# SBUF buffers placed on 128-byte lines, and the convolution layers' weight splits and lateness constants set anew, in a six-layer f32 network on one core

## The chip, the cores and the metric

One core of a Trainium2 chip runs the whole program in one launch. The metric is device time in microseconds (us) of one execution, as the median of several runs.

## The reference

The reference takes 256 tokens of width 1024 in float32 through two blocks. The first has four mixers, in the order convolution (A0), attention (B), short convolution (C), convolution (A1), each around a residual. The second has two layers of a token mixer (M0, M1) and a feed-forward part (F0, F1). The change bears mostly on the convolution mixer:

```python
def conformer_conv_mixer(h, w_in, conv_w, conv_b, ln_g, ln_b, w_out):
    proj = h @ w_in
    val, glu_gate, z = jnp.split(proj, 3, axis=-1)
    u = val * jax.nn.sigmoid(glu_gate)
    u = causal_depthwise_conv(u, conv_w) + conv_b      # 31 taps, 2048 channels
    u = jax.nn.silu(layer_norm(u, ln_g, ln_b))
    return (u * jax.nn.silu(z)) @ w_out
```

## The kernel before

Activations lie with the features on the partitions: a tensor of width 1024 is 8 chunks of 128 partitions by 256 tokens. Every weight matrix is cut into tiles of 128 x 1024, which SP loads into `wr`.

A float32 product is made in one of two ways (`need` and `dense`). **Split**: ACT rounds the tile to `wh` (type fp32r), VectorE or GpSimd subtracts to get the rest `wl`, and TensorE does three fp32r matmuls for each 128 x 256 chunk, `wh` with `hh`, `wh` with `hl` and `wl` with `hh`, where `hh` and `hl` are the same split of the activations. **Native**: the tile is used as loaded, with one float32 matmul for each chunk, which the trace records as two matmul rows (`hn,wr`). A native tile gives ACT, VectorE and GpSimd nothing to do. `NATIVE_A` names the pairs of tiles in a convolution layer that are native: numbers 0 to 15 are the 16 pairs for value and gate, 16 to 23 the 8 pairs for z. Pair 0 is native whatever the table says.

The outputs of a layer come from `Out`: the same three matmuls, with `ph` and `pl` (the split of a layer's inner activations, 8 buffers of 128 x 256) as moving operand, into the PSUM tiles `po`.

In a convolution layer each of the 16 chunks of 128 channels has 31 taps. `POOL_TAPS` says how many of them ACT and GpSimd do: ACT scales a shifted copy into `tap`, GpSimd adds it to `C`. VectorE does the others in PSUM (`po<-U,vec,po`). Then `sums` has TensorE add up `C` and `sq` over the channels, for the layer norm, and only after all 16 chunks can `mean_rstd` (a power on GpSimd, `q`) and with it the layer's output matmuls begin.

The order on each engine isn't written by hand. `program` records operations with a due time (`G.late`, `G.rush`); `Graph.schedule` plays them through a table of estimated durations and takes, for each engine that is free, the ready operation with the earliest due time. Constants such as `CONV`, `SPLIT_LATE`, `LEAD`, `URGENT`, `MOD_LATE` shift due times. Where an operation has two engines to choose from (`FLEX`, for `wl` in the layers named), the planner picks. Where TensorE has nothing ready and too little work in its current stretch, the planner puts in a matmul of zeros, `idle<-idle`, to keep the engine's clock up; `WARM` is a margin of that rule. `Graph.issue` makes the tiles in pools and issues the instructions in the planned order.

```python
        with G.late(-LEAD):
            a.activation(h, w, AF.Copy)
            (dp if flex[0] else v).tensor_tensor(l, w, h.bitcast(F32), op=OP.subtract)
```

`issue` is the helper line of all operations, so every row of the profile has line 494. Here is what the change touches.

Of the kernel before, what the change touches and what calls it, by code (L numbers as in the profile page):

```python
# [8 lines left out]
F32 = mybir.dt.float32  # L9
F32R = mybir.dt.float32r  # L10
BF = mybir.dt.bfloat16
I32 = mybir.dt.int32
# [3 lines left out]

TABLE = {AF.Exp: "exp", AF.Sigmoid: "sigmoid", AF.Silu: "silu", AF.Sin: "sin", AF.Ln: "ln"}
FIFO = 99
DEBUG = []


# [99 lines left out]
class Graph:  # L121
# [87 lines left out]
    def schedule(self):  # L209
# [68 lines left out]
        def blocked(o, e, t):  # L278

            end = t + dict(o.choices)[e]  # L280
            for w, k, i in soon[e]:
                if t < w < end - self.HOLD[1] and w < t + self.HOLD[0] and not ops[i].done and k < o.key[0] - self.HOLD[2] and room(ops[i]) is None:
                    return True
            return False

        def pick(e, t):
# [8 lines left out]
            if e == "ACT":  # L295
                best = None
                for k, i in h:
                    o = ops[i]
                    if o.done:
                        continue  # L300
                    kk = k[0] + (self.TABLE_COST if o.table and o.table != table else 0.0)
                    if best is None or (kk, i) < best[0]:
# [45 lines left out]
        while left or events:  # L348
            for e in ENG:
# [3 lines left out]
                if o is None and e == "PE" and left and self.warm is not None and self.ops[self.warm[1]].done:  # L353
                    if t > latest + 50.0:
                        self.stuck()
                    turn(t)
                    if load >= (self.DOWN if warm else self.UP) + self.WARM:
                        push((tick + 1) * self.TICK + 0.01, "engine", "PE")
# [43 lines left out]
                for j in users[o.i]:  # L402
# [5 lines left out]
                    if waits[j] == 0:  # L408
                        push(max(at[j], t), "ready", w)
                        if w.hurry and e2 in self.HOLDS:  # L410
                            soon[e2].append((max(at[j], t), w.key[0], j))
            if DEBUG and t >= DEBUG[0]:
                DEBUG.pop(0)
                for e in ENG:
# [16 lines left out]
                    break  # L431
        self.time = t

    TABLE_COST = 6.0
    WARM = 0.2
    HOLD = 0.6, 0.1, 5.0
    HOLDS = ("DVE",)

    def idle_op(self, tag):
# [14 lines left out]
    def stuck(self):  # L454
# [5 lines left out]
            lines.append(f"{tag}: {own}")  # L460
        raise RuntimeError("\n".join(lines))


    def issue(self, tc, ctx, pools):
        nc = tc.nc
        ctx.enter_context(tc.manual_schedule())
        made = {n: ctx.enter_context(tc.tile_pool(name=n, bufs=1, **kw)) for n, kw in pools.items()}
        eng = {"PE": nc.tensor, "DVE": nc.vector, "ACT": nc.scalar, "Pool": nc.gpsimd, "DMA": nc.sync}
        count = {}
        for o in self.order:  # L470
            if o.group is not None:
                count[id(o.group)] = count.get(id(o.group), 0) + 1

        def real(a):
            return a.real() if isinstance(a, View) else a
        for o in sorted(self.order, key=lambda o: o.start):
            for b in o.bufs:
                if b.real is None:
                    tag = b.tag if b.slot is None else f"{b.tag}{b.slot}"
                    b.real = made[b.pool].tile(b.shape, b.dtype, name=b.name, tag=tag, bufs=1)  # L480
            if o.fn == "transfer":
                continue
            args = [real(a) for a in o.args]
            kw = {k: real(x) for k, x in o.kw.items()}
            if o.fn == "matmul":
                b = o.outs[0].buf
                kw["start"] = not b.started
                kw["stop"] = True
                b.started = True
                if o.group is not None:  # L490
                    count[id(o.group)] -= 1
                    kw["stop"] = count[id(o.group)] == 0
                kw["skip_group_check"] = True
            getattr(eng[o.eng], o.fn)(*args, **kw)  # L494
# [34 lines left out]
def cost(eng, fn, out, ins, args, kw):  # L529
# [21 lines left out]
    if fn in ("max", "match_replace"):  # L551
# [7 lines left out]
PICKED = -3.0e38  # L559
THRESHOLDS = list(range(1, 17)) + [int(np.ceil(16.0 * 2.0 ** (3.0 * j / 16.0) - 1e-9)) for j in range(1, 16)]  # L560
ALPHA = 4.0 ** 0.25
SLOTS = {"wr": 5, "wh": 6, "wl": 6, "wa": 2, "big": 5, "t1": 8, "t2": 4, "few": 12, "ph": 4, "pl": 4, "pT": 2, "msk": 3,
         "row": 1, "pd": 2, "po": 4, "pa": 2}
RESERVE = {"wr": FIFO, "wh": FIFO, "wl": FIFO, "wa": FIFO, "pd": FIFO}
NATIVE_A = {0, 1, 3, 6, 7, 8, 10, 12, 14, 16, 18, 20, 21}
POOL_TAPS = [2, 13, 9, 11, 14, 12, 8, 17, 19, 9, 9, 12, 9, 10, 17, 27]
LEAD = 4.45
CONV = 33.45
SPLIT_LATE = 37.42
TAIL = 4  # L570
HEADS = 0.0
KA_FIRST = True
URGENT = 7.99
APPLY = 0.0
RAW_C = 1
X_FIRST = 1
X_LATE = 988
WARM = True
SWAP = True
PRELOAD = True  # L580
MOD1 = 'm'
MOD_STEP, MOD_LATE = 4.0, 5
MOD0_STEP, MOD0_LATE = 5.0, 30
ACC_A = set()
ACC_OUT = set()
ACC_LEAD = 3.37
RUSH_TAIL = 0.0
SUMS_LATE = 1.5
LAST_APART = True
FLEX_SUM = True  # L590
FLEX_HL = False
FLEX = "aoc"


def program(G, A, V):
# [68 lines left out]
    def need(src, kind="split"):  # L664
        with G.late(-3 * LEAD):
            w = G.tile("weights", [128, 1024], F32, "wr", "wr")
# [5 lines left out]
        if kind == "acc":  # L672
            with G.late(-LEAD - ACC_LEAD):
                a.activation(h, w, AF.Copy)
# [4 lines left out]
            return [h, l]  # L679
        with G.late(-LEAD):  # L680
            a.activation(h, w, AF.Copy)
# [130 lines left out]
    idle = const([128, 128], "idle", BF)  # L812
    if WARM:
        G.warm = idle, len(G.ops)
# [101 lines left out]
    def residual(out, gain=None, i0=0, late=0.0, raw="split"):  # L916
# [4 lines left out]
        def on_chunk(c, ps, done):  # L921
            with G.rush(URGENT):
                v.tensor_tensor(x[:, c], x[:, c], ps, op=OP.add)
# [8 lines left out]
        if gain:  # L932
            with G.rush(URGENT):
                rr, rs = rms_root(ss)
# [92 lines left out]
    def layer_a(j, raw):  # L1027
# [12 lines left out]
        def conv(c):  # L1040

            u, o = U[:, c % 8], at(C, c)
            b = vc("a_conv_b", j * 16 + c)
            d0 = 31 - POOL_TAPS[c]
            with G.late(CONV):
                if d0 < 31:
# [23 lines left out]
                a.activation(sq, o, AF.Square)  # L1070
                with G.late(-CONV, (), 2.0 if c < 15 else 0.5):
                    sums(st, 0, o, grp, 2048)
# [15 lines left out]
        def kind_of(p):  # L1088
            return "native" if p in NATIVE_A else "acc" if p in ACC_A else "split"

# [11 lines left out]
        G.marks.append(G.last_pe)  # L1102
        with G.rush(URGENT):
            m = mean_rstd(st, 1e-6)
        flex[0] = "o" in FLEX
        out = Out(16)
        for c in range(16):
            n1, n2 = t1("n1"), t1("n2")
            with G.rush(URGENT if c < 2 else 0):
                v.tensor_tensor(n1, at(C, c), m[0], op=OP.subtract)  # L1110
# [55 lines left out]
    def layer_b(raw):  # L1166
# [94 lines left out]
        for gi in range(4):  # L1261
# [15 lines left out]
            for i in range(4):  # L1277
                h = 4 * gi + i
                ps = pair(A["b_in"][h], A["b_in"][16 + h])
                with G.rush(HEADS):  # L1280
                    qk_head(h, ps, (vt, zs))
                    if h < 14:
                        gated(h)
                if h == 15:
                    zgate(2)
                    with G.rush(HEADS):
                        gated(14)
# [56 lines left out]
    def residual_norm(out, l, gi, gain, shift, nxt):  # L1344
# [13 lines left out]
        def on_chunk(c, ps, done):  # L1358
            with G.rush(URGENT):
                v.scalar_tensor_tensor(x[:, c], ps, mod(l, gi, c), x[:, c], op0=OP.mult, op1=OP.add)  # L1360
# [24 lines left out]
    def mixer(l):  # L1385
# [184 lines left out]
        for h in range(4):  # L1570
            with G.rush(HEADS):
                head_b(h)
# [3 lines left out]
        for h in range(4, 8):  # L1576
            with G.rush(HEADS):
                head_b(h)
# [5 lines left out]
        for i in range(8):  # L1584
            gate(i)
            with G.rush(HEADS):
                head_a(i)
# [76 lines left out]
    with G.rush(URGENT):  # L1664
        rr, rs = rms_root(ss)
    with G.late(APPLY):
        rms_apply(rs, "a_norm", 0, SPLIT_LATE)
    raw = m, rr, rs
# [4 lines left out]
    mark()  # L1673
    raw = residual(layer_c(raw), "a_norm", 8, SPLIT_LATE, "native")
    mark()
# [9 lines left out]
def emit(tc, A, V):  # L1685
    G = Graph(SLOTS, RESERVE)
    program(G, A, V)
# [141 lines left out]
```

## Time and profile before

| what | value |
|---|---|
| median of 3 runs | 1830.97 us (1830.06 to 1831.11) |
| the profiled execution, its own time | 1831.1 us |
| its span, first to last instruction | 1829.3 us |
| TensorE matmul busy in the span | 1799.9 us, 98% |
| VectorE, ScalarE, GpSimd busy | 1487.1, 1117.5, 417.6 us |
| mean granted clock of TensorE | 0.991 |

The profiled execution's time is 1.8 us above its span. A matmul's duration in the rows runs from its start to the modelled end of its pipeline, so back-to-back matmuls overlap; what one costs is the distance from its start to the next one's start. The stages by time are: head to 14.7 us, A0 to 249.9, B to 549.9, C to 789.2, A1 to 1013.5, M0 to 1225.1, F0 to 1418.1, M1 to 1628.7, F1 to the end.

### The profile page before, as it was taken

Reading aid. Unit: us, or ns where it says so; the run is one execution under the profiler, and the core shown is the slowest. Engines: PE = TensorE matmul, PEld = TensorE weight load, DVE = VectorE, ACT = ScalarE, POOL = GpSimd, SP = SyncE. Lnnn points to the kernel's source line nnn. Section 1 sums busy time; section 2 is a strip of 40 time slices with the busy share of each in tenths; the row PEclk is TensorE's granted clock in tenths of the full one; section 3 lists DMA queues with packets and bytes.
Section 4 is the critical chain, followed back from the end, with each engine's and each line's share of the span. In section 5 each row is a group of like instructions: output and inputs, shape, how many; then the busy total and the mean of one; then the engine's idle time right before and its main releaser. Section 6 shows DMA issues by size and latency. Waiting matters only on the chain.

```text
span 1829.3 us, 38072 instructions
## 1 busy us (share of the span) xinstructions
PE 1799.9 (98%) x14515; PEld 1725.9 (94%) x14515; DVE 1487.1 (81%) x3260; ACT 1117.5 (61%) x1986; POOL 417.6 (23%) x478
## 2 busy tenths in 40 slices
PE   9999999999999999999999999999999999999999
PEld 8889999999989999999989989999999989999998
DVE  7998988877778676679998798799987685687776
ACT  6777665655544444477775658856555568766554
POOL 4899511001010011049983000010001000000000
PEclk9999999999999999999999999999999999999999
DMA  7344556887754655544445656657885433446661
GB/s 251 116 152 133 184 195 209 263 254 247 246 163 150 185 173 173 174 139 139 139 168 168 214 185 200 223 182 257 289 268 160 151 122 118 137 150 210 194 189 55
DMA packets 107176, 334.95 MB, mean 183 GB/s; under 512 B 12785, under 2 KB 13169, under 8 KB 106993
## 3 DMA queue, kind: packets, MB, share of 16 engines
q1 hardware_dynamic: 106992, 332.52, 56.7%
q8 instruction: 114, 1.87, 0.4%
q14 instruction: 70, 0.57, 0.1%
HBM read 331.43 MB, written 1.05 MB: 182 GB/s over the span
## 4 chain that ended last, share of the span: by engine, by line
PE 79%; DVE 10%; ACT 4%; DMA 2%; POOL 2%; issue 2%; SPq 0%; POOLq 0%; DVEq 0%; ACTq 0%
PE pd L494 49%; PE po L494 22%; PE pa L494 7%; DVE po L494 4%; DVE wl L494 2%; PE idle L494 1%; POOL C L494 1%; ACT wh L494 1%; ACT L494 1%; DMA wa<-in_w_ada 1%; DVE IQ L494 1%; DMA wr<-in_a_in 1%; ACT tap L494 1%; DVE m L494 0%; DMA pi<-in_pos 0%
## 5 line engine op out<-in xcount | busy, mean ns | idle before, releaser
L494 ACT ACTIVATE wh<-wr 128x1024 fp32r<-128x1024 f32 x478 | 502.8, 1058 | 387.0 <-PE pd L494 239.0
L494 PE MATMUL pd<-hh,wh 128*128 128x256 f32 x2456 | 689.7, 283 | 3.6 <-DVE hh L494 1.1
L494 DVE TENSOR_TENSOR wl<-wr,wh 128x1024 fp32r<-128x1024 f32 x458 | 565.4, 1241 | 148.5 <-ACT wh L494 146.3
L494 PE MATMUL pd<-hh,wl 128*128 128x256 f32 x2456 | 678.2, 281 | 1.4 <-POOL wl L494 1.4
L494 PE MATMUL pd<-hl,wh 128*128 128x256 f32 x2456 | 677.9, 280 | 0.3 <-DVE hl L494 0.3
L494 PEld LDWEIGHTS pd<-hh,wh 128*128 128x128 f32 x2456 | 463.8, 189 | 9.3 <-issue 1.7
L494 PEld LDWEIGHTS pd<-hl,wh 128*128 128x128 f32 x2456 | 461.4, 189 | 2.0 <-issue 0.7
L494 PEld LDWEIGHTS pd<-hh,wl 128*128 128x128 f32 x2456 | 459.5, 189 | 3.0 <-POOL wl L494 1.8
L494 POOL TENSOR_TENSOR C<-C,tap 128x233 f32<-128x233 f32 (+15 forms) x364 | 276.0, 784 | 42.2 <-ACT tap L494 32.3
L494 PE MATMUL po<-ph,wh 128*128 128x256 f32 x904 | 254.6, 283 | 0.3 <-DVE ph L494 0.2
L494 PE MATMUL po<-ph,wl 128*128 128x256 f32 x904 | 253.8, 282 | 0.0
L494 PE MATMUL po<-pl,wh 128*128 128x256 f32 x904 | 251.6, 283 | 0.1
L494 DVE SCALAR_TENSOR_TENSOR po<-U,vec,po 128x251 f32<-128x251 f32 (+19 forms) x532 | 217.6, 472 | 2.2
L494 PE MATMUL pd<-hn,wr 128*128 128x256 f32 x768 | 175.2, 382 | 1.3 <-DVE U L494 1.3
L494 PEld LDWEIGHTS po<-ph,wh 128*128 128x128 f32 x904 | 170.2, 188 | 1.2 <-DVE ph L494 0.3
L494 ACT ACTIVATE tap<-U,vec 128x227 f32<-128x227 f32 (+17 forms) x364 | 156.2, 482 | 24.2 <-POOL C L494 16.6
L494 PEld LDWEIGHTS po<-ph,wl 128*128 128x128 f32 x904 | 170.4, 188 | 0.0
L494 PEld LDWEIGHTS po<-pl,wh 128*128 128x128 f32 x904 | 168.9, 189 | 0.4 <-DVE pl L494 0.3
L494 PEld LDWEIGHTS pd<-hn,wr 128*128 128x128 f32 x768 | 142.6, 190 | 19.3 <-DVE U L494 1.6
L494 POOL TENSOR_TENSOR r<-r,neghalf 128x4 f32<-128x4 f32 (+1 forms) x22 | 27.8, 1262 | 302.3 <-DVE r L494 244.9
L494 POOL TENSOR_TENSOR acc<-acc,x 128x256 f32<-128x256 f32 x12 | 9.3, 777 | 336.6 <-DVE x L494 336.0
L494 POOL TENSOR_TENSOR wl<-wr,wh 128x1024 fp32r<-128x1024 f32 x20 | 50.3, 2513 | 154.4 <-ACT wh L494 154.3
(273 smaller groups left out, 2649.7 us busy)
## 6 DMA issues: line engine op xcount, KB each, us to landing
wr<-in_a_in SPq DMA_DIRECT2D x96, 512.0 KB, 3.6
wa<-in_w_ada SPq DMA_DIRECT2D x192, 256.0 KB, 4.0
wr<-in_w_up SPq DMA_DIRECT2D x88, 512.0 KB, 4.4
wr<-in_c_in SPq DMA_DIRECT2D x64, 512.0 KB, 3.6
wr<-in_m_in SPq DMA_DIRECT2D x64, 512.0 KB, 4.1
wr<-in_b_in SPq DMA_DIRECT2D x48, 512.0 KB, 4.5
wr<-in_w_dn SPq DMA_DIRECT2D x44, 512.0 KB, 4.4
wr<-in_a_out SPq DMA_DIRECT2D x32, 512.0 KB, 4.4
```

What stands on the lines that cost most here:

```text
L494: getattr(eng[o.eng], o.fn)(*args, **kw)
```

## The change

`place` makes every tile's row a whole number of 128-byte lines, and a tile of a few words at the head of three pools shifts what follows: the pool of constants by 32 bytes, the weights and the pools behind them by 64 bytes each. The constants, `hh` and `hl` among them, begin 32 bytes behind a line in both programs, and `wr`, `wh`, `wl` 96 bytes behind one in both. `ph` and `pl` begin on a line before (offset 0) and 32 bytes behind one after; the big activation buffers, the `t1` buffers and others move from offset 96 to 32. The reserve `dynamic_dma_scratch_size` falls from 16,384 to 1,024 bytes per partition, which pays for one more `wl` (7) and one more `t2` (5).

`NATIVE_A` has 15 numbers where it had 13; as pair 0 is native anyway, 12 pairs that counted become 15, so in each of the two convolution layers three more pairs (six tiles) are native. `FLEX` is empty: every `wl` is now VectorE's. One more tap of chunk 14 goes to ACT and GpSimd. The rest are due-time constants and margins.

```diff
+LINE = 128
+PHASES = {"const": 8, "weights": 16, "big": 16}
...
-    TABLE_COST = 6.0
-    WARM = 0.2
-    HOLD = 0.6, 0.1, 5.0
+    TABLE_COST = 0
+    WARM = 0.51
+    HOLD = 0.71, 0.14, 5.08
...
+    def place(self, pool, b, tag):
+
+        size = WIDTH[b.dtype]
+        n, line = int(np.prod(b.shape[1:])), LINE // size
+        if b.pool == "psum" or n % line == 0:
+            return pool.tile(b.shape, b.dtype, name=b.name, tag=tag, bufs=1)
+        t = pool.tile([b.shape[0], -(-n // line) * line], b.dtype, name=b.name, tag=tag, bufs=1)[:, :n]
...
+        for n, w in PHASES.items():
+            made[n].tile([128, w], F32, name="phase_" + n, tag="phase", bufs=1)
...
-                    b.real = made[b.pool].tile(b.shape, b.dtype, name=b.name, tag=tag, bufs=1)
+                    b.real = self.place(made[b.pool], b, tag)
...
-SLOTS = {"wr": 5, "wh": 6, "wl": 6, "wa": 2, "big": 5, "t1": 8, "t2": 4, "few": 12, "ph": 4, "pl": 4, "pT": 2, "msk": 3,
-         "row": 1, "pd": 2, "po": 4, "pa": 2}
+SLOTS = {"wr": 5, "wh": 6, "wl": 7, "wa": 2, "big": 5, "t1": 8, "t2": 5, "few": 11, "ph": 4, "pl": 4, "pT": 2, "msk": 3, "row": 1,
+         "pd": 2, "po": 4, "pa": 2}
...
-NATIVE_A = {0, 1, 3, 6, 7, 8, 10, 12, 14, 16, 18, 20, 21}
-POOL_TAPS = [2, 13, 9, 11, 14, 12, 8, 17, 19, 9, 9, 12, 9, 10, 17, 27]
-LEAD = 4.45
-CONV = 33.45
-SPLIT_LATE = 37.42
+NATIVE_A = {1, 3, 4, 6, 7, 8, 9, 10, 12, 14, 16, 18, 19, 20, 21}
+POOL_TAPS = [2, 13, 9, 11, 14, 12, 8, 17, 19, 9, 9, 12, 9, 10, 18, 27]
+LEAD = 3.83
+CONV = 34.01
+SPLIT_LATE = 62.69
...
-HEADS = 0.0
+HEADS = 0.59
...
-URGENT = 7.99
-APPLY = 0.0
+URGENT = 11.55
+APPLY = -1.69
...
-MOD_STEP, MOD_LATE = 4.0, 5
-MOD0_STEP, MOD0_LATE = 5.0, 30
+MOD_STEP = 5.23
+MOD_LATE = 21.72
+MOD0_STEP = 5.0
+MOD0_LATE = 38.22
...
-SUMS_LATE = 1.5
+SUMS_LATE = 2.04
...
-FLEX = "aoc"
+FLEX = ""
...
-    nc = _bacc.Bacc("TRN2", target_bir_lowering=False, num_devices=1)
+    nc = _bacc.Bacc("TRN2", target_bir_lowering=False, num_devices=1, dynamic_dma_scratch_size=1024)
```

Instructions that become more or fewer: 96 float32 matmuls `hn,wr` more, 288 split matmuls `hh,wh`, `hl,wh`, `hh,wl` fewer; 331 fillers `idle<-idle` fewer (851 to 520); 12 `wh` on ACT fewer; `wl` on GpSimd 20 to 0 and on VectorE 458 to 466. By stage the fillers in the order go from 56 to 87 in the head; in A0 from 74 to 3 up to the last projection matmul and from 135 to 19 behind it; in B from 70 to 0; in C from 55 to 83; in A1 from 32 to 2 and from 138 to 21; and from 291 to 305 in M0, F0, M1, F1 and the tail together.

The order on TensorE in A0 where the projection ends and the output matmuls begin, before (`pa<-cst,C` and `pa<-cst,sq` are the sums of the last convolution chunk, `pa<-cst,r` and `q` the layer norm's rows, `po<-ph` the first output matmul):

```order
L494 MATMUL pa<-cst,C 128x1 x2
L494 LDWEIGHTS idle
L494 MATMUL idle<-idle 128x128
...
L494 MATMUL pa<-cst,sq_2658 128x1 x2
...
L494 MATMUL pa<-cst,r 128x128 x2
...
L494 MATMUL pa<-cst,q 128x128 x2
...
L494 MATMUL po<-ph,wh 128x256
```

and the same place now:

```order
L512 MATMUL pa<-cst,C 128x1 x2
L512 MATMUL pd<-hh,wh 128x256
L512 MATMUL pa<-cst,sq_2240 128x1 x2
L512 MATMUL pd<-hl,wh 128x256
...
L512 MATMUL pa<-cst,r 128x128 x2
L512 MATMUL pd<-hh,wh 128x256
...
L512 MATMUL pa<-cst,q 128x128 x2
L512 MATMUL pd<-hl,wh 128x256
...
L512 MATMUL po<-ph,wh 128x256
```

Where only fillers stood between the last sums and the first output matmul, there are now 27 split matmuls of the last z pair (`pd`), and 19 fillers behind them.

The order on GpSimd in the middle of A0's projection, before (`C<-C,tap` are the convolution's additions):

```order
L494 TENSOR_TENSOR C<-C,tap 128x228
L494 TENSOR_TENSOR wl<-wr,wh 128x1024
L494 TENSOR_TENSOR C<-C,tap 128x227
L494 TENSOR_TENSOR C<-C,tap 128x240
L494 TENSOR_TENSOR C<-C,tap 128x226
...
L494 TENSOR_TENSOR C<-C,tap 128x235
L494 TENSOR_TENSOR wl<-wr,wh 128x1024
L494 TENSOR_TENSOR C<-C,tap 128x234
```

and now:

```order
L512 TENSOR_TENSOR C<-C,tap 128x228
L512 TENSOR_TENSOR C<-C,tap 128x242
L512 TENSOR_TENSOR C<-C,tap 128x227
L512 TENSOR_TENSOR C<-C,tap 128x241
L512 TENSOR_TENSOR C<-C,tap 128x226
L512 TENSOR_TENSOR C<-C,tap 128x240
```

The subtractions for `wl` that stood between the additions are gone from GpSimd.

## Rows read from the trace of the kernel before

**Rows 1.** The page, busy time and share of each engine.
```profile
PE 1799.9 (98%) x14515; PEld 1725.9 (94%) x14515; DVE 1487.1 (81%) x3260; ACT 1117.5 (61%) x1986; POOL 417.6 (23%) x478
```

**Rows 2.** Busy by stage: window, us, PE, PEld, DVE, ACT, POOL, clock, DMA, GB/s.
```profile
14.70:185.60 170.90, 165.99 (x1109) 153.03 (x1106) 161.29 (x361) 130.70 (x287) 150.86 (x186) 1.00 0.48 157
185.60:198.30 12.70, 10.70 (x157) 9.89 (x156) 10.04 (x20) 4.31 (x8) 6.06 (x5) 1.00 0.65 223
249.90:549.90 300.00, 296.54 (x2361) 280.06 (x2360) 245.05 (x584) 162.79 (x274) 28.32 (x22) 0.99 0.73 233
789.20:954.00 164.80, 164.49 (x1084) 153.47 (x1083) 156.00 (x361) 126.24 (x285) 144.79 (x183) 1.00 0.45 144
954.00:968.30 14.30, 11.65 (x152) 10.85 (x151) 10.41 (x22) 6.20 (x9) 3.27 (x5) 0.88 0.71 261
```

**Rows 3.** The same stages, fillers (tile idle) alone: us, PE, PEld, DVE, clock, DMA, GB/s.
```profile
14.70:185.60 170.90, 7.26 (x74) 5.14 (x74) 0.00 (x0) 1.00 0.48 157
185.60:198.30 12.70, 8.89 (x135) 8.11 (x135) 0.00 (x0) 1.00 0.65 223
249.90:549.90 300.00, 9.20 (x70) 5.68 (x71) 0.00 (x0) 0.99 0.73 233
789.20:954.00 164.80, 2.83 (x32) 2.09 (x33) 0.00 (x0) 1.00 0.45 144
954.00:968.30 14.30, 10.56 (x138) 9.84 (x138) 0.00 (x0) 0.88 0.71 261
```

**Rows 4.** Timeline of PE at A0's changeover: start, us, operation, count, idle before.
```profile
188.46 3.83 PE L494 MATMUL idle<-idle 128*128 128x128 bf16 x62
193.41 0.58 PE L494 MATMUL pa<-cst,C 128*128 128x1 f32 x4 [1.12 <-DVE C L494]
...
198.32 0.38 PE L494 MATMUL po<-ph,wh 128*128 128x256 f32 x1 [0.17 <-DVE ph L494]
```

**Rows 5.** The same at A1's changeover.
```profile
963.40 0.58 PE L494 MATMUL pa<-cst,C 128*128 128x1 f32 x4 [0.19 <-DVE C L494]
...
968.33 0.36 PE L494 MATMUL po<-ph,wh 128*128 128x256 f32 x1
```

**Rows 6.** Tile wl by stage: us, PE, PEld, DVE, POOL, clock, DMA, GB/s.
```profile
14.70:185.60 170.90, 44.61 (x176) 30.80 (x176) 23.40 (x18) 17.63 (x7) 1.00 0.48 157
789.20:954.00 164.80, 44.61 (x176) 30.89 (x176) 26.53 (x18) 10.84 (x4) 1.00 0.45 144
```

**Rows 7.** The page's costliest groups: a tap's addition, and the subtraction for wl.
```profile
L494 DVE TENSOR_TENSOR wl<-wr,wh 128x1024 fp32r<-128x1024 f32 x458 | 565.4, 1241 | 148.5 <-ACT wh L494 146.3
...
L494 POOL TENSOR_TENSOR C<-C,tap 128x233 f32<-128x233 f32 (+15 forms) x364 | 276.0, 784 | 42.2 <-ACT tap L494 32.3
```

**Rows 8.** Timeline of PE in A1: native stretches of 32 and 48 recorded rows.
```profile
805.70 7.07 PE L494 MATMUL pd<-hn,wr 128*128 128x256 f32 x32
...
824.80 10.52 PE L494 MATMUL pd<-hn,wr 128*128 128x256 f32 x48
```

**Rows 9.** Timeline of PE, F0's end: first and last of 48 matmuls in a row.
```profile
1405.98 0.28 PE L494 MATMUL po<-ph,wh 128*128 128x256 f32 x1
...
1411.50 0.28 PE L494 MATMUL pd<-ph,wl 128*128 128x256 f32 x1
```

**Rows 10.** Timeline of PE, M0's output: first and last of 81 matmuls in a row.
```profile
1203.83 0.28 PE L494 MATMUL po<-hl,wh 128*128 128x256 f32 x1
...
1212.89 0.28 PE L494 MATMUL po<-hh,wh 128*128 128x256 f32 x1
```

**Rows 11.** Timeline of PE, A1's last projection: first and last of 28 matmuls in a row.
```profile
943.81 0.28 PE L494 MATMUL pd<-hl,wh 128*128 128x256 f32 x1
...
946.99 0.28 PE L494 MATMUL pd<-hh,wh 128*128 128x256 f32 x1
```

**Rows 12.** The page, DMA queue of the loads: packets, MB, share of 16 engines.
```profile
q1 hardware_dynamic: 106992, 332.52, 56.7%
...
wr<-in_a_in SPq DMA_DIRECT2D x96, 512.0 KB, 3.6
```

More of the change, by code (lines that the diff above doesn't have):

```diff
@@ L18 @@
 FIFO = 99
+LINE = 128
+PHASES = {"const": 8, "weights": 16, "big": 16}
+WIDTH = {F32: 4, F32R: 4, I32: 4, BF: 2}
 DEBUG = []
@@ L461, in stuck @@
         raise RuntimeError("\n".join(lines))
+    def place(self, pool, b, tag):
[4 more added lines that the diff above has]
+        t = pool.tile([b.shape[0], -(-n // line) * line], b.dtype, name=b.name, tag=tag, bufs=1)[:, :n]
+        names = [f"a{i}" for i in range(len(b.shape) - 1)]
+        if len(names) == 1:
+            return t
+        return t.rearrange(f"p ({' '.join(names)}) -> p {' '.join(names)}", **dict(zip(names[1:], b.shape[2:])))
     def issue(self, tc, ctx, pools):
@@ L586 @@
 ACC_LEAD = 3.37
-RUSH_TAIL = 0.0
-SUMS_LATE = 1.5
+RUSH_TAIL = 0
+SUMS_LATE = 2.04
 LAST_APART = True
```

## Prediction
> **What bounds the kernel now.** I read the page's busy shares first. TensorE's matmuls are busy 98% of the span, the next engine 81% [rows 1], so the kernel ends when TensorE has got through its list, and a change is worth what it does to that list and to TensorE's waits. But 851 of the 14,515 matmul rows are fillers, work on zeros where nothing was ready. So the second view is the table of stages, once with everything and once with the fillers alone. A stage's time without use is its length minus the busy time, plus the fillers [rows 2, 3]:
>
> - A0's projection: 170.9 - 166.0 + 7.3 = 12.2 us.
> - A0's changeover to the output matmuls: 12.7 - 10.7 + 8.9 = 10.9 us.
> - B: 300.0 - 296.5 + 9.2 = 12.7 us.
> - A1's projection: 164.8 - 164.5 + 2.8 = 3.1 us; its changeover: 14.3 - 11.7 + 10.6 = 13.2 us.
>
> Together 52 us. The third view, TensorE's timeline at the changeovers, says who is late: 62 fillers run for 3.8 us, then TensorE still waits 1.1 us for VectorE's finished `C`, and the first output matmul comes at 198.32, 4.9 us after the last sums at 193.41 [rows 4]. In A1 it is 963.40 to 968.33, again 4.9 us behind a `C` [rows 5]. So the end of the convolution sets the changeover. The convolution in turn runs through GpSimd, which is busy 150.9 of 170.9 us in A0's projection and 144.8 of 164.8 in A1's [rows 2], most of it in additions of 784 ns each [rows 7]. Of that, 17.6 us (7 tiles) and 10.8 us (4 tiles) aren't convolution at all: they are `wl` subtractions that the planner gave to GpSimd [rows 6].
>
> **The change part by part,** against the profiled execution's 1831.1 us, which lies 0.1 us above the median of the runs.
>
> *Changeovers.* No `wl` goes to GpSimd any more. The last convolution chunk then ends 17.6 - 0.8 (one more addition [rows 7]) = 16.8 us earlier in A0, near 176.6, and 10.0 us earlier in A1, near 953.4. Counted to the same start, the projection in A0 would end at 185.6 - 12.2 + 4.2 = 177.6 (the last term is the native tiles, below), in A1 at 954.0 - 3.1 + 4.2 = 955.1. From the convolution's end the 4.9 us chain has to run, so 3.9 us in A0 and 3.2 us in A1 would stay open with nothing else; the order has 19 and 21 fillers there, at 62 ns [rows 4] 1.2 and 1.3 us. I take 2 us for each and gain (10.9 - 2) + (13.2 - 2) = 20.1 us. Bounds: 1.2 and 1.3 us left gives 21.6, 3.9 and 3.2 left gives 17.0. [...]
>
> *VectorE as cover.* It takes over the `wl`. In A0's projection it and GpSimd made 18 + 7 = 25 of them [rows 6]; six tiles become native, so some 19 are left, one more than VectorE had: 1.2 us [rows 7] on an engine that is busy 161.3 of 170.9 [rows 2]. In A1 it is 22 - 6 = 16 for 18. This hides, but with under 9 us of air in A0; if it did not, the taps that VectorE does would end the convolution instead.
>
> *Waits inside the projections and B.* The fillers fall from 74 to 3, 32 to 2 and 70 to 0 in the order. I count the fillers' 7.3, 2.8 and 9.2 us as gone, and of the further waiting (4.9, 0.3 and 3.5 us) two thirds in A0, where some of it was for a `wl` of GpSimd, and none in B: 10.5 + 2.6 + 9.2 = 22.3 us. Bounds: all of it, 28.0; half of the fillers, 9.7, if other waits step into their places. In the other stages the fillers go from 346 to 388 beside the head, 2.6 us at 62 ns; `WARM` alone asks for more of them in the same gap, so I take 0, and 2.6 us for the upper end. The head's own count says nothing, as it waits for the first loads.
>
> *Native tiles.* The second native stretch has 16 recorded rows more than the first and takes 3.45 us more [rows 8]: 431 ns for two rows, one float32 matmul. A pair has 16 of these, 6.90 us. Split, it has 48 matmuls. They come at two paces: 9.06 us over 80 steps, 113.3 ns, in M0 [rows 10], and 3.18 over 27, 117.8 ns, in A1 [rows 11]; a pair is 5.44 or 5.65 us. Six pairs more are 7.5 to 8.8 us dearer. I take 8.4, since the convolution layers are where the slow pace was seen. This is certain work on the bounding engine; what it buys is counted above.
>
> *Address of `ph` and `pl`.* They are the moving operand of 904 x 3 output matmuls and 72 x 3 in the mixers, 2928 in all. They run at 5.52 us over 47 steps, 117.4 ns [rows 9]. The output matmuls of M0, same PSUM tiles, same weight buffers, but with `hh` and `hl` as moving operand, run at 113.3 [rows 10]. What sets these apart is that `hh` lies 64 bytes from the weights modulo 128 and `ph` 32; after the change `ph` lies as `hh` does. At M0's pace that is 2928 x 4.1 = 12.0 us; but `hh` has stretches at 117.8 too [rows 11], where it would be 0. I take three quarters, 9 us.
>
> [...]
>
> *Everything else* at nothing: the big buffers, `t1` and small tiles move their addresses, but their users are VectorE, ACT and GpSimd, off the end except as above; ACT does 12 `wh` less.
>
> Sum: 20.1 + 22.3 + 9.0 - 8.4 = 43.0 us. 1831.1 - 43.0 = **1788 us**, 2.3% less.
>
> **Rivals.**
>
> 1. *The address does nothing.* For it: `hh` at 117.8 ns with the favourable address [rows 11]. Against it: 80 steps without one slow stretch in M0 [rows 10]. Time: 1788 + 9 = 1797 us. This is also the way in which the change doesn't do what it says.
> 2. *The convolution still ends late.* VectorE's two-input subtractions and taps, now all on one engine with 9 us to spare, end the convolution instead of GpSimd, and fillers come back at the changeovers: 1788 + 20 = 1808 us. For it: the 161.3 us of VectorE [rows 2]. Against it: the exchange of `wl` costs it 1.2 us at most.
> 3. *Slower: loads run one at a time.* The change cuts the DMA reserve in SBUF sixteenfold. If the loads' descriptors went through it and only one load fitted, each would be awaited alone. A 512 KB tile takes 3.6 us from issue to landing [rows 12], and 332.5 MB are some 634 such tiles: 2280 us, some 450 more than now. The point from which it decides is two loads in flight: at 3.6 us for two, a tile comes each 1.8 us, and a split tile keeps TensorE for 24 x 113.3 = 2.7 us. For it: nothing in the trace shows what the reserve holds. Against it: all loads are issued by SP and run on a hardware queue [rows 12]. [...]
>
> **How the numbers follow.** The forecast gets 0.72, rival 1 0.13, rival 2 0.08, rival 3 0.04; 0.03 is left for gains that other waits eat up. A measurement can tell 0.2%, 3.7 us, from no change. Forecast and rivals 1 and 2 are all faster by more than that: 0.93, and a hair more from the rest gives 0.94; within it 0.02; slower 0.04. The low end takes the best of each bound: 21.6 + 28.0 + 12.0 - 7.5 = 54.1, 1777 us; I go 3 us further for stretches at 1.2 GHz inside B (its clock is 0.99 [rows 2]). The high end: 17.0 + 9.7 + 0 - 8.8 - 2.6 = 15.3, 1816 us, needs all that is bad at once; I stop at 1806, which takes in rival 1 and all but the edge of rival 2.
>
> **What would show it.** Right: in both changeovers under 3 us from the last `pd` matmul to the first `po`, hardly any fillers before them, GpSimd free of `wl`, and output matmuls with `ph` near 113 ns in stretches. The address is wrong if they stay at 117. The forecast as a whole is wrong if the wait for `C` stands at the changeovers as before, or if TensorE's rows show waits for a `wl` of VectorE or for loads in the conv layers, where the order has no filler to give.

## The result, and the profile after

The changed kernel takes 1810.25 us (median of 4 runs, 1806.01 to 1812.58) where the kernel before, on the same chip, takes 1830.85 (1830.06 to 1831.11): a ratio of 0.9882, 95% interval 0.9860 to 0.9903. It is faster, but by 20.6 us and not by the 43 of the forecast, and 4 us above the range. On a second chip the same kernel took 1799.51 us, a ratio of 0.9824 (0.9772 to 0.9876); how far its runs spread is part of the explanation.

The page's first part of the changed kernel, to be held against [rows 1]:

```profile
PE 1792.4 (99%) x14088; PEld 1722.9 (95%) x14088; DVE 1483.2 (82%) x3264; ACT 1102.9 (61%) x1975; POOL 363.6 (20%) x462
```

TensorE has 427 matmuls fewer, but its busy time fell by only 7.5 us. Next, the stages of [rows 2] (window, us, then busy time of PE, PEld, DVE, ACT, POOL, then clock, DMA share, GB/s); A0's projection, its changeover, B, A1's projection, its changeover:

```profile
14.70:184.10 169.40, 169.40 (x1024) 156.01 (x1023) 160.33 (x375) 125.36 (x286) 135.07 (x184) 0.99 0.49 165
184.10:185.21 1.11, 1.11 (x19) 1.03 (x18) 1.07 (x4) 1.11 (x3) 0.00 (x0) 1.00 0.14 52
236.90:531.50 294.60, 289.75 (x2268) 274.59 (x2267) 238.79 (x567) 161.89 (x275) 27.68 (x22) 1.00 0.71 231
773.80:940.80 167.00, 167.00 (x1015) 154.10 (x1014) 157.86 (x373) 124.53 (x285) 135.33 (x184) 1.00 0.49 155
940.80:942.18 1.38, 1.38 (x24) 1.31 (x22) 1.34 (x5) 1.38 (x4) 0.00 (x0) 1.00 0.77 125
```

The same windows with the fillers alone, as in [rows 3] (PE, PEld, DVE, clock, DMA share, GB/s):

```profile
14.70:184.10 169.40, 0.33 (x3) 0.25 (x3) 0.00 (x0) 0.99 0.49 165
184.10:185.21 1.11, 0.95 (x16) 0.90 (x16) 0.00 (x0) 1.00 0.14 52
236.90:531.50 294.60, 0.00 (x0) 0.00 (x0) 0.00 (x0) 1.00 0.71 231
773.80:940.80 167.00, 0.28 (x2) 0.20 (x2) 0.00 (x0) 1.00 0.49 155
940.80:942.18 1.38, 1.12 (x19) 1.06 (x19) 0.00 (x0) 1.00 0.77 125
```

By the prediction's own rule (length minus busy, plus fillers) the time without use is now 0.3, 1.0, 4.9, 0.3 and 1.1 us: 7.6 us where it was 52. That is 44 us less, and with 8.4 us taken off for the dearer native tiles some 36 us should remain, but the kernel is only 20.6 us shorter. So the waits went as forecast, and something took time back while TensorE was busy. TensorE's timeline around the changeovers (start, us, operation, count) shows the first half of that; it answers to [rows 4, 5]:

```profile
179.74 0.50 PE L512 MATMUL pa<-cst,C 128*128 128x1 f32 x4
...
184.26 1.07 PE L512 MATMUL idle<-idle 128*128 128x128 bf16 x16
185.21 0.36 PE L512 MATMUL po<-ph,wh 128*128 128x256 f32 x1
...
936.43 0.50 PE L512 MATMUL pa<-cst,C 128*128 128x1 f32 x4
...
941.06 1.24 PE L512 MATMUL idle<-idle 128*128 128x128 bf16 x19
942.18 0.35 PE L512 MATMUL po<-ph,wh 128*128 128x256 f32 x1
```

The sums over `C` now lie inside the projection and wait for nothing; one group of fillers of 1.1 or 1.2 us is left. The second half is in the same view at the end of M0, the stretch of [rows 10], and at the end of F0, that of [rows 9] (first and last of 197 and of 49 matmuls in a row):

```profile
1164.76 0.28 PE L512 MATMUL po<-hh,wl 128*128 128x256 f32 x1
...
1187.85 0.28 PE L512 MATMUL po<-hh,wh 128*128 128x256 f32 x1
...
1382.08 0.28 PE L512 MATMUL po<-ph,wl 128*128 128x256 f32 x1
...
1387.73 0.28 PE L512 MATMUL pd<-ph,wl 128*128 128x256 f32 x1
```

M0's matmuls now come 23.09 us / 196 = 117.8 ns apart, where they came 113.3 apart; those of F0 5.65 / 48 = 117.7, where it was 117.4. The new addresses did not bring `ph` to the pace of `hh`: they brought `hh` to the pace of `ph`.

To judge that over a whole execution and not over one stretch, I took every pair of neighbouring recorded split matmuls of 256 columns without a wait between them, over 9,000 of 10,560 (before: 10,848), and averaged the distance from start to start, apart for `hh`, `hl` and for `ph`, `pl` as moving operand. "Slow" is the share of steps of 117 ns or more. "Distance" is the address of the weights minus that of the moving operand, modulo 256 bytes; the 32 that the prediction has for `ph` is the 96 of this table, modulo 128 and counted the other way.

| kernel | hh: distance wh/wl | ns, slow | ph: distance wh/wl | ns, slow |
|---|---|---|---|---|
| before | 64/64 | 114.8, 30% | 96/96 | 117.8, 70% |
| changed | 192/192 | 117.6, 95% | 192/192 | 117.1, 85% |

Modulo 128, which is all that the prediction looked at, `hh` is at 64 in both kernels and `ph` comes to 64: by that view only `ph` changes. Modulo 256 `hh` went from 64 to 192. With 7632 split matmuls on `hh` and 2928 on `ph` the difference is 7632 x 2.83 - 2928 x 0.64 ns = 19.7 us more.

### The profile page after: what moved, and what is told of

It reads as the page before. It is cut to its first block, busy times and chain, and to the rows that moved or that the text cites. A ratio compares the mean times of both kernels' runs of the same rounds, so it can differ in the third digit from the quotient of the medians.

```text
span 1810.8 us, 37129 instructions
## 1 busy us (share of the span) xinstructions
PE 1792.4 (99%) x14088; PEld 1722.9 (95%) x14088; DVE 1483.2 (82%) x3264; ACT 1102.9 (61%) x1975; POOL 363.6 (20%) x462
## 4 chain that ended last, share of the span: by engine, by line
PE 88%; DVE 6%; DMA 3%; ACT 2%; issue 1%; POOL 0%; SPq 0%; ACTq 0%; DVEq 0%; POOLq 0%
PE pd L512 59%; PE po L512 21%; PE pa L512 8%; DMA wa<-in_w_ada 2%; DVE wl L512 1%; PE idle L512 1%; DVE wa L512 1%; ACT L512 0%; ACT wh L512 0%; DVE x L512 0%; DMA wr<-in_a_in 0%; DVE hn L512 0%; DVE IQ L512 0%; DVE hh L512 0%; DVE nm L512 0%
## 5 line engine op out<-in xcount | busy, mean ns | idle before, releaser
L512 PE MATMUL pd<-hh,wh 128*128 128x256 f32 x2360 | 670.0, 286 | 3.0 <-DVE up L512 2.1
L512 PE MATMUL pd<-hh,wl 128*128 128x256 f32 x2360 | 660.2, 283 | 0.0
L512 PEld LDWEIGHTS pd<-hh,wh 128*128 128x128 f32 x2360 | 445.5, 189 | 5.8 <-ACT wh L512 2.0
L512 PEld LDWEIGHTS pd<-hl,wh 128*128 128x128 f32 x2360 | 443.1, 189 | 1.6 <-issue 0.5
L512 POOL TENSOR_TENSOR C<-C,tap 128x230 f32<-128x230 f32 (+16 forms) x366 | 269.0, 758 | 47.0 <-ACT tap L512 35.2
L512 DVE SCALAR_TENSOR_TENSOR po<-U,vec,po 128x255 f32<-128x255 f32 (+19 forms) x530 | 216.4, 471 | 2.2
L512 PE MATMUL pd<-hn,wr 128*128 128x256 f32 x960 | 214.7, 381 | 0.0
L512 PEld LDWEIGHTS pd<-hn,wr 128*128 128x128 f32 x960 | 179.8, 190 | 23.0
L512 ACT ACTIVATE tap<-U,vec 128x226 f32<-128x226 f32 (+17 forms) x366 | 155.3, 479 | 17.3 <-POOL C L512 8.1
L512 DVE CUSTOM_DVE_ANT_0 wa<-wa,scr,mods 128x512 f32<-128x512 f32 x96 | 72.1, 751 | 14.1 <-DMA wa<-in_w_ada 13.5
```

## The experiments

**The two halves apart, and two shifts of the weights.** First the kernel before with the new addresses alone:

```diff
+PHASES = {"const": 8, "weights": 16, "big": 16}
+        for n, w in PHASES.items():
+            made[n].tile([128, w], F32, name="phase_" + n, tag="phase", bufs=1)
-                    b.real = made[b.pool].tile(b.shape, b.dtype, name=b.name, tag=tag, bufs=1)
+                    b.real = self.place(made[b.pool], b, tag)
-    nc = _bacc.Bacc("TRN2", target_bir_lowering=False, num_devices=1)
+    nc = _bacc.Bacc("TRN2", target_bir_lowering=False, num_devices=1, dynamic_dma_scratch_size=1024)
```

> The kernel before with the new addresses alone (lines of 128 bytes, the three shifts, the small DMA reserve); plan and order as before. Theory A, the distance from the weights to the moving operand hh, hl, modulo some power of two above 128, sets the pace of the split matmuls: hh falls to about 117.5 ns as in the changed kernel, and the time rises by some 15 to 22 us to 1846 to 1853. Theory B, the new order sets the pace and the addresses do nothing: about 1831, hh near 114.8 ns on average as before. Theory C, the other buffers that moved to hh's own offset disturb it: also 1846 to 1853.

Then the changed kernel with the old addresses (the same lines taken back, but for the reserve):

> The changed kernel without the new addresses (no lines, no shifts), with its plan, order, slots and small DMA reserve. Theories A and C: hh back near 114.8 ns on average, ph at 117.8, time 1785 to 1795. Theory B: hh at 117.5 ns and 1808 to 1812 as the changed kernel.

And the changed kernel with the weights 896 or 128 bytes further on, `"weights": 240` or `48` in place of 16 words in `PHASES`. Each puts the weights 64 bytes modulo 256 from `hh`, and leaves them 192 from `ph`:

> The changed kernel with the weights, and all that lies behind them, 896 bytes further on, so that weights minus hh is the same modulo 1024 as before the change; ph stays at its new distance to the weights. Theory A: hh near 114.8 ns, ph at 117 to 118 ns, time 1786 to 1796. Theories B and C: hh at 117.5 ns, 1806 to 1813.

> The changed kernel with the weights, and all that lies behind them, 128 bytes further on: weights minus hh is then 64 modulo 256 as before the change, but 64 and not 320 modulo 512. Theory A with modulo 256: hh near 114.8 ns and 1786 to 1796. Theory A with modulo 512 or more, and theories B and C: hh at 117.5 ns, 1806 to 1813.

| kernel | us | ratio to before, 95% | hh ns, slow | ph ns, slow |
|---|---|---|---|---|
| addresses alone | 1841.42 | 1.0044 (1.0015 to 1.0073) | 117.0, 83% | 117.0, 82% |
| plan alone | 1798.23 | 0.9814 (0.9759 to 0.9869) | 115.2, 39% | 117.8, 71% |
| weights +896 | 1800.15 | 0.9824 (0.9776 to 0.9873) | 115.0, 35% | 117.1, 83% |
| weights +128 | 1797.22 | 0.9810 (0.9761 to 0.9858) | 115.0, 35% | 117.2, 85% |

The kernel before took 1832.33 beside these. The plan alone gives 34.1 us; the addresses alone cost 9.1. That is less than the 15 to 22 us expected for a pace like the changed kernel's, which `hh` nearly has here: in the profiled execution the split matmuls, counted from each start to the next and without waits, took 14.2 us more than before, while fillers and waits took 8.5 us less. A slower stream partly fills time that TensorE had nothing for. The shifted kernels keep the plan and the form of the weight buffers, and within one execution `hh` at 64 has 35% slow steps and `ph` at 192 has 83 to 85%. The distance modulo 128 is the same 64 for both, so that isn't what counts. One stretch, though, says little. Here is the end of M0 in TensorE's timeline, first of the addresses alone, then of the plan alone:

```profile
1194.84 0.28 PE L513 MATMUL po<-hl,wh 128*128 128x256 f32 x1
...
1217.92 0.28 PE L513 MATMUL po<-hh,wl 128*128 128x256 f32 x1
```

```profile
1154.83 0.28 PE L510 MATMUL po<-hh,wl 128*128 128x256 f32 x1
...
1177.92 0.28 PE L510 MATMUL po<-hh,wh 128*128 128x256 f32 x1
```

Both are 197 matmuls in 23.1 us, 117.8 ns, though the second has the old, good distance, with which the kernel before ran the same place at 113.3 [rows 10]. At 64 and 192 the address sets how often a stream is slow, not whether it is (in the table above, 35 to 39% of the steps at 64 and 82 to 85% at 192).

**The distance varied.** The changed kernel unaltered, and with other words in `PHASES` (`"tmp"` moves `ph` and `pl`):

```diff
-PHASES = {"const": 8, "weights": 16, "big": 16}
+PHASES = {"const": 8, "weights": 48, "big": 16, "tmp": 32}
...
+PHASES = {"const": 8, "weights": 64, "big": 16, "tmp": 40}
...
+PHASES = {"const": 8, "weights": 24, "big": 16, "tmp": 48}
```

> The changed kernel once more, as the yardstick for the three variants beside it on the same chip. Expected: 1806 to 1813, split matmuls with hh at 117.5 ns, with ph at 117. Theory C (distance of 192 bytes modulo 256 between weights and moving operand makes the slow pace) and its rivals agree here.

> The changed kernel with weights minus hh and weights minus ph both 64 modulo 256 (weights 128 bytes further on, the pool of ph another 128). If the distance modulo 256 alone sets the pace, hh stays near 114.9 ns as with the weights moved alone, ph falls from 117 to 113.5 to 115.5 ns, and the time is 5 to 10 us under the run with the weights moved alone: 1787 to 1793. If ph is slow for another reason (its pool, the output stage), ph stays at 117 and the time at 1795 to 1800.

> The changed kernel with weights minus hh 128 and weights minus ph 32 modulo 256: two distances not yet seen. If what counts is that the two reads keep away from each other's line, 128 should be as fast as 64 or faster (hh 113 to 115 ns, total 1790 to 1800). If the pace depends on the distance in another way, hh is 117 ns or more and the time 1806 to 1815. For ph at 32 no forecast beyond 113 to 120 ns.

> The changed kernel with weights minus hh 224 and weights minus ph 0 modulo 256. In the kernel before, rawh at distance 0 ran at 120 ns in few samples; if that is the distance, ph is near 120 ns here, 8 us more in all. hh at 224: near the slow 192, so 117 to 118 ns. Time 1810 to 1822. If hh is faster than 116 ns, the slow distances are a narrow band around 192.

| kernel | us | ratio to before, 95% | hh: distance, ns, slow | ph: distance, ns, slow |
|---|---|---|---|---|
| changed, again | 1799.51 | 0.9824 (0.9772 to 0.9876) | 192, 116.3, 66% | 192, 115.7, 52% |
| both at 64 | 1795.04 | 0.9793 (0.9771 to 0.9816) | 64, 115.6, 49% | 64, 115.1, 37% |
| 128 and 32 | 1821.27 | 0.9942 (0.9922 to 0.9963) | 128, 118.8, 82% | 32, 118.2, 66% |
| 224 and 0 | 1813.11 | 0.9897 (0.9872 to 0.9922) | 224, 117.3, 62% | 0, 119.7, 99% |

Same instructions, same order, 26 us between the best and the worst: the address matters. The unaltered kernel was less often slow here than in its first profile, and 10.7 us faster in the median: its share of slow steps isn't the same in two profiled executions (of two chips). Its own runs here reach from 1789.0 to 1812.0. `ph` came down with its distance, from 85% slow with the weights moved alone to 37%. Two times lie above the range expected for their paces, both at 64 by 2 us, 128 and 32 by 6. At distances other than 64 and 192 the steps don't fall into two groups (`ph` in the kernel before, at 96, has 11 to 23% of its steps at each whole ns from 115 to 120), so there the mean says more than the share.

**Air behind each weight buffer.** One more idea was that buffers exactly 4096 bytes apart were the trouble. The changed kernel with 128 bytes of air behind each `wr`, `wh` and `wl`, which alternates the distance from buffer to buffer, and two with the start moved so that all distances are 16 bytes off the multiples of 64:

```diff
+        if b.pool == "weights" and b.tag in ("wr", "wh", "wl"):
+            return pool.tile([b.shape[0], 1056], b.dtype, name=b.name, tag=tag, bufs=1)[:, 0:1024]
...
+            return pool.tile([b.shape[0], 1056], b.dtype, name=b.name, tag=tag, bufs=1)[:, 4:1028]
...
+            return pool.tile([b.shape[0], 1056], b.dtype, name=b.name, tag=tag, bufs=1)[:, 28:1052]
```

> The changed kernel with 32 words of air behind each weight buffer, so that weights minus hh is 64 modulo 256 for every second buffer and 192 for the others, in one execution. Theory A (the distance modulo 256 sets the pace): matmuls from the buffers at 64 run at 114 to 115 ns on average, those at 192 at 117 ns or more. Theory D (both distances have two stable paces, 113.3 and 117.8 ns, and which one a stream falls into is decided by its start and not by the address): no difference between the two kinds of buffer beyond 0.5 ns, long stretches of either pace that run over both. Time 1790 to 1810 under both.

> The same buffers with the weights 16 bytes on: distance to hh and ph 80 modulo 128 instead of 64. If 64 sits at the edge of a conflict and 80 is beyond it, the slow stretches go: 113.3 ns throughout and 1775 to 1788. If 64 is the best point, 80 lies between it and the 117.8 seen at 96: 115.5 to 118 ns and 1803 to 1815.

> The same buffers with the weights at distance 48 modulo 128 from hh and ph. If 64 sits at the edge of a conflict on the other side, the slow stretches go here: 113.3 ns throughout and 1775 to 1788. If 64 is the best point, 115.5 to 118 ns and 1803 to 1815.

> The kernel before, unchanged, for one more profile on another chip. Theory A: hh again near 114.8 ns, time 1828 to 1834. Theory D: the share of slow stretches differs from the first profile's 31%, and the time with it: 7632 matmuls by the change of the mean.

| kernel | us | ratio to before, 95% | distance wh; wl | hh ns, slow | ph ns, slow |
|---|---|---|---|---|---|
| 128 bytes of air | 1781.91 | 0.9725 (0.9684 to 0.9766) | 64; 64 and 192 | 113.9, 10% | 113.9, 9% |
| distance 80 | 1814.12 | 0.9907 (0.9877 to 0.9937) | 80; 80 and 208 | 118.4, 78% | 118.4, 81% |
| distance 48 | 1819.79 | 0.9932 (0.9910 to 0.9953) | 176; 48 and 176 | 118.6, 76% | 118.5, 77% |

The kernel before, profiled once more, took 1832.64 us with 30% slow steps on `hh`. The first of the three is 28.3 us under the changed kernel's first median and 17.6 under its second, and 8 us under what either theory had expected; the one at distance 48 came out 5 us above its slow case. In it `wh` fell on 64 in all buffers used and `wl` mostly on 192, which I hadn't planned.

**Which part of that is it?** The changed kernel with `wl` alone moved, so that `wh` is at 192 and `wl` at 64; with 256 bytes of air, so that all stays at 192 but the spacing is no longer 4096; and the 128 bytes of air in the kernel with the new addresses and the old plan:

```diff
+        if b.pool == "weights" and b.tag == "wl":
+            return pool.tile([b.shape[0], 1088], b.dtype, name=b.name, tag=tag, bufs=1)[:, 32:1056]
...
+        if b.pool == "weights" and b.tag in ("wr", "wh", "wl"):
+            return pool.tile([b.shape[0], 1088], b.dtype, name=b.name, tag=tag, bufs=1)[:, 0:1024]
```

> The changed kernel with every wh (and wr) at 192 and every wl at 64 modulo 256 from hh and ph. Theory E: a stream of split matmuls has two paces, 113.3 and 117.8 ns; at one constant distance either of them lasts once begun, and a change of the distance from one weight load to the next (64 to 192 or back) throws the stream out of the slow one. Then here, where each wl changes it: mean pace 113.3 to 114.5 ns, slow share under 15%, 1776 to 1786. Theory F: what helped was that the weight buffers no longer stand 4096 bytes apart; here wh and the next wh stand 8448 apart, so it helps too, and this run alone does not part E from F. If 192 is simply a slow distance: 1795 to 1805.

> The changed kernel with 256 bytes of air behind each weight buffer instead of 128: buffers 4352 bytes apart, all at 192 modulo 256. Theory E: no change of distance modulo 256, so the slow pace lasts as in the changed kernel: mean 116 to 117.6 ns, slow share 55 to 95%, 1795 to 1812. Theory F (the spacing of 4096 was the trouble): mean under 114.5 ns and 1776 to 1786, as with 128 bytes of air.

> The kernel before, with its plan and order, the new addresses and 128 bytes of air behind each weight buffer (distances 64 and 192 mixed). Theory E or F: the pace of hh and ph falls to 113.5 to 114.5 ns; against the kernel before, 7632 x 0.8 + 2928 x 3.8 ns = 17 us less: 1811 to 1820. If the fast pace needs the new order, 1825 to 1845.

The first took 1793.96 us, ratio 0.9792 (0.9746 to 0.9839), 36% slow: changing distances from one matmul to the next doesn't by itself keep a stream fast. The second took 1807.01, 0.9853 (0.9810 to 0.9896), 74% slow: the spacing of 4096 isn't the trouble. The third took 1824.56, 0.9960 (0.9941 to 0.9980), against 1.0044 with the same plan and addresses without air: between its two expectations. Its two streams differ: `hh` ran at 114.4 ns with 19% slow, `ph` at 116.8 with 65%. With the old plan's number of buffers the air falls out differently. In this program 84% of the matmuls of `wh` with `hh` and `hl` have `wh` at 64, and 84% of those of `wl` have it at 192; with `ph` and `pl` it is the reverse, `wh` at 192 in 83% and `wl` at 64 in 82%. So the pairing helped under the old plan as well, where it was met. What stood was the pairing, `wh` at 64 and `wl` at 192, and the last experiment tries it alone, in every buffer.

**The pairing alone, and two parts of the plan taken back from it.**

```diff
-PHASES = {"const": 8, "weights": 16, "big": 16}
+PHASES = {"const": 8, "weights": 48, "big": 16, "tmp": 32}
...
+        if b.pool == "weights" and b.tag == "wl":
+            return pool.tile([b.shape[0], 1088], b.dtype, name=b.name, tag=tag, bufs=1)[:, 32:1056]
```

> The changed kernel with every buffer of high parts (wh) 64 bytes and every buffer of low parts (wl) 192 bytes from hh, hl, ph and pl modulo 256. Theory G (what counts is the distance modulo 256, wh at 64 and wl at 192, which were the pairings with 6 to 14% of slow steps in the two runs that had them): the mean step with hh is 113.4 to 114.0 ns, slow steps under 15%, time 1775 to 1783 us. Rival (the gain of the run with 128 bytes of air came from the mixing of distances from buffer to buffer, not from this pairing): the stream goes back to 114.7 to 115.5 ns, time 1785 to 1798 us.

Measured: 1782.37 us, ratio 0.9741 (0.9723 to 0.9759), 113.9 ns with 8% slow on `hh` and 113.9 with 9% on `ph`. The pairing gives what the air gave, without the mixing. In TensorE's timeline the end of F0, which stood at 117.7 ns in the changed kernel, has the same 48 steps in 5.48 us, 114.2 ns:

```profile
1360.99 0.28 PE L514 MATMUL po<-ph,wl 128*128 128x256 f32 x1
...
1366.47 0.28 PE L514 MATMUL pd<-ph,wl 128*128 128x256 f32 x1
```

What the pairing does to a stream, the traces show too. I divided TensorE's rows into unbroken runs of at least 12 steps with `hh` and `hl`, or with `ph` and `pl`, as moving operand, and compared the mean of a run's first three steps with that of its last six, calling it slow from 115.5 ns on:

| kernel, distance wh/wl | runs | began slow | of these, ended fast |
|---|---|---|---|
| pairing, 64/192 | 193 | 92 | 92 |
| both at 64, 64/64 | 193 | 130 | 35 |
| before, `hh` alone, 64/64 | 129 | 102 | 74 |
| `wl` alone moved, 192/64 | 191 | 105 | 37 |
| changed, 192/192 | 190 | 180 | 0 |
| changed, again, 192/192 | 193 | 106 | 1 |
| addresses alone, 192/192 | 197 | 152 | 0 |

With the pairing every run that began slow turned fast within its first 11 steps; with all at 192 next to none did. In none of these kernels did a run that began fast end slow. How many begin slow varies even between two profiles of the changed kernel; what the address decides here is whether matmuls that begin at 117.8 ns get out of it.

This version and the one with 128 bytes of air are the fastest here, below both the kernel before and the changed one. On the pairing kernel I then took back the rule for GpSimd, and in another kernel the table of native pairs:

```diff
-FLEX = ""
+FLEX = "aoc"
...
-NATIVE_A = {1, 3, 4, 6, 7, 8, 9, 10, 12, 14, 16, 18, 19, 20, 21}
+NATIVE_A = {0, 1, 3, 6, 7, 8, 10, 12, 14, 16, 18, 20, 21}
```

> The kernel of j0_wh_64_wl_192 with the old rule that GpSimd may take a share of the low parts; its order has 17 of them there, and 693 filler matmuls in place of 520. Theory of the prediction (GpSimd's low parts hold up the convolution, so that TensorE waits for C at the changeovers): the fillers of the two changeovers are back and the time is 8 to 20 us above j0_wh_64_wl_192. Rival (only the new costs and due times matter): within 4 us of j0_wh_64_wl_192.

> The kernel of j0_wh_64_wl_192 with the old table of fp32 pairs (384 fp32 matmuls, 8.4 us less matmul work by the prediction's term), so that more weight blocks are split on VectorE. If the added fp32 tiles are pure cost: 6 to 10 us below j0_wh_64_wl_192. If they pay by relieving ScalarE and VectorE of splits, whose waits come back without them: 4 to 16 us above it, with more fillers in the trace.

They took 1800.45 us (0.9844, 0.9825 to 0.9864) and 1800.58 (0.9841, 0.9825 to 0.9858), each 18 us above the pairing kernel at the same pace of matmuls (113.9 ns, 8 to 10% slow). The costliest groups of the fillers and of GpSimd's `wl` (busy us, mean ns, idle before), with the pairing, with GpSimd's rule back, and with the old native pairs:

```profile
L514 PE MATMUL idle<-idle 128*128 128x128 bf16 x520 | 42.3, 228 | 2.0 <-DVE zero L514 1.0 <-DVE x L514 1.0
```

```profile
L514 PE MATMUL idle<-idle 128*128 128x128 bf16 x693 | 58.9, 230 | 3.8 <-ACT hd L514 1.1 <-DVE zero L514 1.0 <-DVE C L514 0.8
...
L514 POOL TENSOR_TENSOR wl<-wr,wh 128x1024 fp32r<-128x1024 f32 x17 | 41.5, 2443 | 160.0 <-ACT wh L514 160.0
```

```profile
L514 PE MATMUL idle<-idle 128*128 128x128 bf16 x764 | 66.3, 230 | 3.3 <-ACT hd L514 1.1 <-DVE zero L514 1.0 <-DVE x L514 0.8
```

With GpSimd's rule back the fillers grow by 16.6 us, the larger part of the 22.6 between the two profiled executions (1804.65 and 1782.07 us; the medians are 18 apart). A0's changeover in TensorE's timeline of that kernel shows the old picture:

```profile
185.84 0.61 PE L514 MATMUL idle<-idle 128*128 128x128 bf16 x8 [0.84 <-DVE C L514]
186.28 0.56 PE L514 MATMUL pa<-cst,C 128*128 128x1 f32 x4
...
191.41 0.35 PE L514 MATMUL po<-ph,wh 128*128 128x256 f32 x1 [0.90 <-DVE ph L514]
```

The wait for `C` is there again, and the first output matmul comes 5.1 us after the sums; the changeovers, from the last projection matmul to the first output matmul, are 9.6 and 4.4 us long in place of the pairing kernel's 1.0 and 1.1. With the old native pairs the fillers grow by 24.0 us, while the remaining matmul work falls by 5.3 (busy time 1759.7 to 1778.4, less the fillers). Counted from each start to the next and without waits, the native matmuls take 41.9 us less and the split ones with `hh` and `hl` 33.7 more, so 8.2 us of work are saved. The native tiles are dearer on TensorE and still pay; the 12 blocks that ScalarE and VectorE then needn't split are the likely reason, though the planner's order changes with them. Each part is worth 18 us where the other is in place. How much of the plan's 34 us the two give together, with both taken back at once, was not tried.

## Why the prediction was wrong

**The step that failed is the term "Address of `ph` and `pl`", 9 us of gain.** It had two faults. It took `hh` at 64 bytes modulo 128 for the good case and saw that `ph` would come to lie the same; but the change moved `hh` too, from 64 to 192 modulo 256, and the term counted no cost for that. The addresses alone made the kernel 9.1 us longer where the sum had a gain of 9. In the changed kernel's first profile `ph` gave 1.9 us and `hh` cost 21.6, which is the 19.7 above, and the prediction's own sign for this came: `ph` stayed at 117.1 ns. The gain itself was there at another address: with the pairing `ph` runs at 113.9, by the means 11.4 us less than before. The other fault is that it rested on one stretch for each case: 80 steps at 113.3 ns [rows 10] against 47 at 117.4 [rows 9], though [rows 11] had one with `hh` at 117.8. The three quarters that I took hedged the size, not the sign. The range's upper end took the address at 0 and no worse; no row of the profile excluded a loss, so it should have had one. The low end's 3 us for stretches at 1.2 GHz inside B name a frequency that no run shows: the traces have a granted share of the clock alone, 0.99 in B before and 1.00 now. Nor was it tried whether the fillers keep that share up; over the span it was 0.991 with 851 of them and 0.994 with 520.

**The plan's terms held.** Their sum was 34.0 us; the plan alone gave 34.1, with an interval of the ratio that lets it be 24 to 44. That the two agree to 0.1 us is luck: in its profile `hh` ran 0.4 ns slower than before, some 3 us that the plan had to make up.

- *Changeovers*: 20.1 forecast. Time without use there went from 10.9 + 13.2 to 1.0 + 1.1: 22.0. The bound of 1.2 and 1.3 us left was the true one. That GpSimd's `wl` were a cause is shown by taking its rule back.
- *VectorE as cover*: it made 20 and 18 `wl` in the two projections, I had 19 and 16; in the two projections TensorE has no time without use beyond 0.3 us, so the cover held.
- *Waits inside the projections and B*: 22.3 forecast (by its own words, with A1's 2.8 us of fillers whole, it adds up to 22.6); 28.0 went to 5.5, a gain of 22.5. In B the further waits even grew, from 3.5 to 4.9.
- *Native tiles*: 8.4 forecast; the work saved with the old table was 8.2 from start to start. That they buy waits elsewhere was right, and worth more than I could see.

**The rivals.** Rival 1, that the address does nothing, named a time that many runs came near (1797), but as a mechanism it is refuted: the same matmuls ran from 113.9 to 119.7 ns on the mean, with the distance of the two operands. Rival 2 named a time, 1808 us, close to the 1810 measured, but that is chance: the changeovers of the changed kernel refute its mechanism. Rival 3 is refuted by the DMA rows, where a 512 KB tile still lands after 3.6 us, as in [rows 12]:

```profile
wr<-in_a_in SPq DMA_DIRECT2D x96, 512.0 KB, 3.6
```

**What stays open.** Why matmuls that begin at 117.8 ns speed up with one distance of each kind and not with 192 alone, and why they begin at that pace, nothing here tells. Nor was it tried which of the two parts of the pairing matters more on `ph`, or whether pairings outside multiples of 64 do as well. The lateness constants and `WARM` were not tried by themselves.

## What to carry to other kernels

When a change moves buffers, list every operand pair of the bounding engine before and after, modulo more than one power of two, and price those that lose as well as those that gain. Judge a pace over all steps of an execution, never over one stretch. Where matmuls run back to back on a bounding TensorE, try the weights' offset as a parameter: here, by the ratios to the kernel before, the pairing took 15 to 26 us from the changed kernel without one instruction more or less.

## What the runs showed of the hardware

With the operands 64 or 192 bytes apart modulo 256, these float32r matmuls of 128 x 256 run at one of two paces, 113.3 and 117.8 ns. With all at 192 an unbroken stream keeps the pace that it begins with (579 of the 580 runs in the table above); with the pairing a slow one turns fast (92 of 92). Other distances have other paces: `ph` in the kernel before, at 96, has no step under 115 ns, and at 0 82% of the steps with `ph` take 120. In the changed kernel's timeline of TensorE, A1's last projection runs at 117.7 (47 steps in 5.53 us), and its output, after the changeover, at 113.2 (53 in 6.00), both at distance 192:

```profile
930.78 0.28 PE L512 MATMUL pd<-hh,wl 128*128 128x256 f32 x1
...
936.31 0.28 PE L512 MATMUL pd<-hl,wh 128*128 128x256 f32 x1
...
943.96 0.28 PE L512 MATMUL po<-ph,wh 128*128 128x256 f32 x1
...
949.96 0.28 PE L512 MATMUL po<-ph,wl 128*128 128x256 f32 x1
```

The windows of these two stretches (columns as in the stages above) have a granted clock of 1.00 each, so the clock isn't the cause. Nor is the traffic of the loads: the slow one has 364 GB/s, the fast one 133, but a straight-line fit over all steps of that execution gives under 0.5 ns between no traffic and full traffic (in the kernel before, on `hh`, about 1 ns less with it).

```profile
930.78:936.50 5.72, 5.72 (x51) 5.72 (x50) 4.99 (x8) 3.59 (x6) 0.00 (x0) 1.00 0.97 364
943.96:950.10 6.14, 6.14 (x57) 6.14 (x56) 6.14 (x11) 4.29 (x7) 2.35 (x3) 1.00 0.48 133
```

The share of slow steps by distance modulo 256 was: `wh` 64 with `wl` 192, 8 to 10%; `wh` 192 with `wl` 64, 25 to 40%; all 64, 30 to 49%; all 192, 52 to 95%; 96, 70 to 71%; 0, 99%, and there the mean was 119.7 ns. The kernel before took 1819 to 1842 us over the chips used here and the changed one 1789 to 1813, while the pairing kernel kept within 1778 to 1785 in its four runs. That fits layouts which leave the pace of a stream to how it begins, but the runs without a profile don't show their paces.
